# Branch s, the output projection and the feed-forward by two groups of 516 tokens; gate and up tile together as a 2x2 block product of seven; the down projection in two parts

## The chip, the cores and the metric

The kernel runs on one core of one Trainium2 chip. The metric is the device time of one execution in microseconds (us), as the median of several runs. Names of engines as the profile has them: PE (TensorE matmul), PEld (its weight loads), DVE (VectorE), ACT (ScalarE), POOL (GpSimd), SP (SyncE, which issues the DMAs here).

## What is computed

One decoder layer for 1024 prompt tokens and 8 sample tokens, float32, width 1024. Cut to what the change touches:

```python
z = x @ w_in                              # branches a (RG-LRU), s (window attention), c (memory attention), gates g
merged = sum(gates[:, :, n] * (br @ w_branch[n]) for n, br in enumerate((a_out, s_out, c_out)))
h = layer_norm(ALPHA * x + merged @ w_out, ln1_g, ln1_b)
gt, up = jnp.split(h @ w_gate_up, 2, axis=-1)            # 2816 + 2816 features: 22 + 22 tiles of 128
h = layer_norm(ALPHA * h + (jax.nn.silu(gt) * up) @ w_down, ln2_g, ln2_b)
```

## The kernel before, in words

Activations lie transposed: features on the 128 partitions, the T = 1032 tokens (1024 + 8) along the columns. A tile of features by all tokens is thus 128 x 1032. To keep float32 accuracy each operand is split into a high part (ACT casts it, L71) and a low part (DVE subtracts, L72), and each product of a 128x128 weight block with some columns is three matmuls: high x high, high x low, low x high (`mm3`, L105 to L107). Weights come as halves of 128 x 512 floats through a ring of six raw buffers (`half_raw`, SP issues the DMA), and are split into a ring of five high and four low halves (`half_pair`).

The front half, `project`, computes `x @ w_in` in 30 units. Each unit takes two tiles of 128 features as a 2x2 block product with seven products in place of eight (`fast_quarter`, `fast_step`, L244 to L246): the blocks are two halves of the input features and two halves of the tokens, and the pieces are 258 columns wide. While memory attention and window attention run, the branch products of a and c are filled in between as jobs (`branch`, `product`). These products go by three chunks of columns, CH = 384, 384 and 264.

The back half, about 1076 us into the span, works as follows before the change.

- *Branch s* (`brs`, L105 to L107): eight output tiles, each 8 weight blocks x 3 terms x 3 chunks. Its operands `bs` are read back from DRAM (`scr_s`) into slots of their own, so that they can be loaded and split while branch c still runs. Each result is gated, added to M and split (`mH`, `mL`).
- *Output projection* (`out_proj`, `op`): chunk by chunk over all eight tiles, with `wout` split once and kept (`resident`). The first layer norm (`n1`) of a chunk runs in two steps inside the next chunk: the column mean by a matmul with ones (`col_mean`), eight differences (L906), eight squares on ACT and seven sums (L910), a second mean, the root on ACT (L914), the reciprocal (L917), eight scalings (L919). `emit` then writes high and low part of h (L1022, L1023).
- *Feed-forward* (`ffn`): in parts of 8, 7 and 7 feature tiles. For each tile and chunk a gate product (`fg`), tanh, an up product (`fu`) and their product, split into `gH`, `gL`, which stay in memory until the part's down product (`d`) adds them to `acc`. The last part's down weights are resident; there the second layer norm (`n2`) runs chunk by chunk, the last one in a form of its own (`last_layer_norm`, `dl`), which shifts the mean out by small matmuls (`shift`, L959, L960).

A tile framework builds the program: code order gives the order of each engine, with moves by a scheduler, and pools decide when a buffer is free. The order rows below show its outcome.

Of the kernel before, what the change touches and what calls it, by code (L numbers as in the profile page):

```python
# [18 lines left out]
P = 128  # L19
D = 1024  # L20
# [8 lines left out]
FPARTS = ((0, 8), (8, 7), (15, 7))  # L29
NORM_AT = (0, 3)  # L30
LATE = 4
LAST_CH = ((0, 0, 384), (1, 0, 384), (2, 0, 264))
# [9 lines left out]
)  # L42
THIRDS = ((0, 344), (344, 344), (688, 344))
# [10 lines left out]
class Builder:  # L54
# [72 lines left out]
    def setup(self):  # L127
# [10 lines left out]
        nc.vector.memset(self.shift.bitcast(F32), -2.0 / 256)  # L138
# [445 lines left out]
    def product(self, step, br, m, c, wb, gate):  # L584

        nc = self.nc
        t0, n = CH[c]
        ps = self.mm_tile(wb, self.act[br], c, f"br{br}{m}_{c}")
        t = gate[:, t0:t0 + n]
        dst = self.M[m][:, t0:t0 + n]  # L590
        if step == 0:
            nc.vector.scalar_tensor_tensor(dst, t, 1.0, ps, op0=ALU.add, op1=ALU.mult)
            return
        nc.vector.scalar_tensor_tensor(t, t, 1.0, ps, op0=ALU.add, op1=ALU.mult)
        nc.vector.tensor_add(dst, dst, t)
        if step == 2:
            hi, lo = (self.slot(e, c, f"m{e}{m}_{c}", 0) for e in "HL")
            self.split(hi, lo, dst)
            self.merged[m][c] = (hi, lo)
# [262 lines left out]
    def resident(self, src, nk, name, which):  # L862

        nc = self.nc
        raws = [self.half_raw(src[:, o:min(o + 512, nk * P)], min(512, nk * P - o), f"{name}r{o}")
                for o in range(0, nk * P, 512)]
        out = []
        for c in range(3):
            k0, k1 = 3 * c, min(3 * c + 3, nk)
            n = (k1 - k0) * P  # L870
            hi, lo = (self.slot(e, c, f"{name}{e}{c}", which, n) for e in "HL")
            for e, raw in enumerate(raws):
                a, b = max(k0, 4 * e), min(k1, 4 * e + 4)
                if a < b:
                    o = slice((a - k0) * P, (b - k0) * P)
                    self.split(hi[:, o], lo[:, o], raw[:, (a - 4 * e) * P:(b - 4 * e) * P])
            out += [(hi[:, i * P:(i + 1) * P], lo[:, i * P:(i + 1) * P]) for i in range(k1 - k0)]
        return out

    def mm_res(self, w, act, c, name, tag="mm"):  # L880
        n = CH[c][1]
        ps = self.bank(tag, name)
        self.mm3(ps[:, :n], [(w[k], act[k][c]) for k in range(len(w))])
        return ps[:, :n]

    def col_mean(self, s, n, name):

        nc = self.nc
        hi = self.ph.tile([P, 384], F32R, tag="lh", name=f"{name}h", bufs=1)[:, :n]
        lo = self.ph.tile([P, 384], F32R, tag="ll", name=f"{name}l", bufs=1)[:, :n]  # L890
        self.split(hi, lo, s)
        ps = self.bank("o", f"{name}p")[:, :n]
        nc.tensor.matmul(ps, self.ones, hi, start=True, stop=False)
        nc.tensor.matmul(ps, self.ones, lo, start=False, stop=True)
        return ps

    def layer_norm(self, c, r, s1, gcol, emit, name, late=False):


        nc, ph = self.nc, self.ph  # L900
        n = r[0].shape[1]
        yield
        mu = self.col_mean(s1, n, f"{name}mu{c}")
        s2 = ph.tile([P, 384], F32, tag="s2", name=f"{name}s2{c}", bufs=1)[:, :n]
        for m in range(KT):
            nc.vector.tensor_sub(r[m], r[m], mu)  # L906
            sq = s2 if m == 0 else ph.tile([P, 384], F32, tag="sq", name=f"{name}sq{c}_{m}", bufs=2)[:, :n]
            nc.scalar.activation(sq, r[m], AF.Square)
            if m:
                nc.vector.tensor_add(s2, s2, sq)  # L910
        yield
        var = self.col_mean(s2, n, f"{name}va{c}")
        rs = ph.tile([P, 384], F32, tag="rs", name=f"{name}rs{c}", bufs=1)[:, :n]
        nc.scalar.activation(rs, var, AF.Sqrt, bias=self.vec[:, V_EPS:V_EPS + 1])  # L914
# [16 lines left out]

    def last_layer_norm(self, n, r, product, gcol, emit):


        nc, ph = self.nc, self.ph
        ones = self.ones.bitcast(F32)
        tile_ = lambda tag, name, bufs, dt=F32: ph.tile([P, 384], dt, tag=tag, name=name, bufs=bufs)[:, :n]
        s1, s2 = tile_("s1", "ls1", 1), tile_("s2", "ls2", 1)
        hi, lo = (ph.tile([P, n], F32R, tag=f"c0{e}", name=f"c0{e}", bufs=1) for e in "hl")
        e1, e2 = self.bank("t", "le1")[:, :n], self.bank("t", "le2")[:, :n]  # L940

        def account(m):
            sq = s2 if m == 0 else tile_("sq", f"lsq{m}", 2)
# [10 lines left out]
        for m in range(KT):  # L954
# [6 lines left out]
            nc.vector.scalar_tensor_tensor(r[m], ps, 0.5, r[m], op0=ALU.mult, op1=ALU.add)  # L961
            if m == 1:
                s = tile_("xres", "lc0", 3)
                nc.vector.tensor_add(s, r[0], r[1])
                self.split(hi, lo, s)
            elif m == LATE - 1:
# [4 lines left out]
                for k in range(LATE):  # L971
                    nc.vector.scalar_tensor_tensor(r[k], c0, 0.5, r[k], op0=ALU.mult, op1=ALU.add)
# [7 lines left out]
        mu, rs = tile_("xres", "lmu", 3), tile_("gt", "lrs", 3)  # L980
# [12 lines left out]
    def out_proj(self, merged):  # L993
        nc, io, ph = self.nc, self.io, self.ph
        self.accs = [self.acc.tile([P, T], F32, tag="acc", name=f"acc{m}", bufs=8) for m in range(KT)]
        h = [[None] * 3 for _ in range(KT)]
        self.norm = None
        w = [None] * KT
        for c, (t0, n) in enumerate(CH):
            s1 = ph.tile([P, 384], F32, tag="s1", name=f"o1s{c}", bufs=1)[:, :n]  # L1000
            rs = []
            for m in range(KT):
                if c == 0:
                    w[m] = self.resident(io["wout"][m], KT, f"wo{m}", 1)
                ps = self.mm_res(w[m], merged, c, f"op{m}_{c}", tag=("mm", "s")[m % 2])
                if m in NORM_AT:
                    self.norm_step()
                xr = ph.tile([P, 384], F32, tag="xres", name=f"xres{m}_{c}", bufs=3)[:, :n]
                nc.sync.dma_start(xr, io["xT"][:, m, t0:t0 + n])
                nc.scalar.mul(xr, xr, ALPHA)  # L1010
                r = self.accs[m][:, t0:t0 + n]
                nc.vector.scalar_tensor_tensor(r, ps, 0.5, xr, op0=ALU.mult, op1=ALU.add)  # L1012
                if m == 1:
                    nc.vector.tensor_add(s1, rs[0], r)
                elif m > 1:
                    nc.vector.tensor_add(s1, s1, r)
                rs.append(r)

            def emit(m, v, c=c):
                bias = self.vec[:, V_B1 + m:V_B1 + m + 1]  # L1020
                hi, lo = (self.slot(e, c, f"h{e}{m}_{c}", 0) for e in "HL")
                nc.scalar.activation(hi, v, AF.Identity, bias=bias)  # L1022
                nc.vector.scalar_tensor_tensor(lo, v, bias, hi.bitcast(F32), op0=ALU.add, op1=ALU.subtract)  # L1023
                nc.gpsimd.tensor_scalar(v, v, bias, ALPHA, op0=ALU.add, op1=ALU.mult)
                h[m][c] = (hi, lo)
# [252 lines left out]
```

## Time and profile before

| | |
|---|---|
| median of 3 runs | 2028.45 us (2027.67, 2028.92, 2028.45) |
| span of the profiled execution | 2027.6 us |
| busy PE, DVE, ACT, POOL | 1963.3, 1204.2, 879.1, 125.3 us |
| mean granted clock of PE | 0.991 |
| branch c ends, branch s begins | 1075.93, 1077.21 us |
| last product of the down projection begins | 2010.25 us |

The page gives busy times of one execution. A PE that is 97% busy says that matmuls bound the whole; which of them, and what a pause costs, stands in the windows, the waits and the timeline. In a timeline row the columns are start, duration, engine, line, operation, output from inputs, shape and count, and in brackets the idle time before and what ended it. Durations of neighbouring matmuls overlap, so the pace is read from start to start.

### The profile page before, as it was taken

The page shows a single profiled execution, that of the slowest core. Times are in us where ns is not written, and L with a number is a line of the kernel's source. Part 1 is how long each engine was busy: PE and PEld are TensorE (multiplying, and loading weights), DVE is VectorE, ACT ScalarE, POOL GpSimd, SP SyncE. Part 2 cuts the span into 40 slices and gives each one's busy share as a digit, 9 for nine tenths or more (in the row PEclk, how much of TensorE's full clock was granted, in tenths as well). Part 3 has the DMA queues.
Part 4 walks back from the last instruction along what each step waited for, and adds up shares of the span by engine and source line. Part 5 has one row for each costly group of instructions (what it writes and reads, how often), then busy time and mean ns, then how long its engine had stood idle before and what let it go on. Part 6 is the DMA issues. An engine that isn't in the chain of part 4 may idle for free.

```text
span 2027.6 us, 35380 instructions
## 1 busy us (share of the span) xinstructions
PE 1963.3 (97%) x13732; PEld 1930.0 (95%) x13732; DVE 1204.2 (59%) x2565; ACT 879.1 (43%) x1922; POOL 125.3 (6%) x164
## 2 busy tenths in 40 slices
PE   6899999999999999999999999999999999999997
PEld 5899999999999898988999999999999999999996
DVE  8597888777676555389886568533322332223357
ACT  5456565555656455388774244422201221122324
POOL 3000010100000000012110003100000000000001
PEclk8999999999999999999999999999999999999999
DMA  4365455462333676567525241111211111111102
GB/s 173 129 227 181 153 186 170 144 228 82 118 131 114 234 240 215 158 170 204 155 72 174 85 145 30 43 42 43 58 47 43 42 57 41 57 45 43 56 28 84
DMA packets 140439, 235.41 MB, mean 116 GB/s; under 512 B 17280, under 2 KB 69584, under 8 KB 140240
## 3 DMA queue, kind: packets, MB, share of 16 engines
q1 hardware_dynamic: 140272, 233.17, 36.2%
q8 instruction: 107, 1.75, 0.4%
q14 instruction: 60, 0.49, 0.1%
HBM read 179.95 MB, written 55.23 MB: 116 GB/s over the span
## 4 chain that ended last, share of the span: by engine, by line
PE 86%; DVE 6%; DMA 3%; ACT 3%; issue 1%; SPq 0%; ACTq 0%; DVEq 0%; POOL 0%; POOLq 0%
PE ub L245 5%; PE ub L244 5%; PE ub L246 5%; PE fg L105 4%; PE fg L106 4%; PE fg L107 4%; PE fu L107 4%; PE fu L105 4%; PE fu L106 4%; PE d L105 3%; PE d L107 3%; PE d L106 3%; PE ud L246 2%; PE ud L245 2%; PE ud L244 2%; PE brs L105 1%
## 5 line engine op out<-in xcount | busy, mean ns | idle before, releaser
L105 PE MATMUL fg<-hH,wfg_h 128*128 128x384 f32 (+1 forms) x528 | 168.3, 319 | 3.0 <-DVE acc L1012 1.7
L106 PE MATMUL fg<-hL,wfg_h 128*128 128x384 f32 (+1 forms) x528 | 167.7, 318 | 0.4 <-DVE hL L1023 0.4
L107 PE MATMUL fu<-hH,wfu_l 128*128 128x384 f32 (+1 forms) x528 | 167.7, 318 | 0.0
L106 PE MATMUL fu<-hL,wfu_h 128*128 128x384 f32 (+1 forms) x528 | 167.6, 317 | 0.0
L105 PE MATMUL fu<-hH,wfu_h 128*128 128x384 f32 (+1 forms) x528 | 167.5, 318 | 0.0
L107 PE MATMUL fg<-hH,wfg_l 128*128 128x384 f32 (+1 forms) x528 | 167.5, 317 | 0.0
L1041 DVE TENSOR_TENSOR ft<-ft,fu 128x384 f32<-128x384 f32 (+1 forms) x66 | 33.8, 513 | 139.1 <-PE fu L107 139.1
L105 PE MATMUL d<-gH,wd_h 128*128 128x384 f32 (+1 forms) x360 | 114.4, 318 | 0.0
L106 PE MATMUL d<-gL,wd_h 128*128 128x384 f32 (+1 forms) x360 | 114.2, 317 | 0.0
L107 PE MATMUL d<-gH,wd_l 128*128 128x384 f32 (+1 forms) x360 | 114.2, 317 | 0.0
L1039 DVE SCALAR_TENSOR_TENSOR ft<-ft,fg 128x384 f32<-128x384 f32 (+1 forms) x66 | 33.8, 513 | 135.2 <-ACT ft L1038 132.9
L71 ACT CAST gH<-ft 128x384 fp32r<-128x384 f32 (+1 forms) x66 | 31.7, 481 | 175.0 <-DVE ft L1041 175.0
L105 PEld LDWEIGHTS fg<-hH,wfg_h 128*128 128x128 f32 x528 | 99.1, 188 | 3.9 <-DVE acc L1012 2.0
L106 PEld LDWEIGHTS fg<-hL,wfg_h 128*128 128x128 f32 x528 | 99.2, 188 | 1.0 <-DVE hL L1023 0.9
L107 PEld LDWEIGHTS fg<-hH,wfg_l 128*128 128x128 f32 x528 | 99.3, 188 | 0.0
L107 PEld LDWEIGHTS fu<-hH,wfu_l 128*128 128x128 f32 x528 | 99.2, 188 | 0.0
L105 PEld LDWEIGHTS fu<-hH,wfu_h 128*128 128x128 f32 x528 | 99.2, 188 | 0.0
L106 PEld LDWEIGHTS fu<-hL,wfu_h 128*128 128x128 f32 x528 | 99.2, 188 | 0.0
L1061 DVE SCALAR_TENSOR_TENSOR acc<-d,acc 128x384 f32<-128x384 f32 (+1 forms) x48 | 24.8, 516 | 108.4 <-PE d L107 108.4
L1038 ACT ACTIVATE ft<-fg 128x384 f32<-128x384 f32 (+1 forms) x66 | 30.1, 456 | 134.8 <-PE fg L107 134.8
L244 PE MATMUL ub<-th,u_0h 128*128 128x258 f32 x240 | 69.4, 289 | 7.5 <-ACT th L71 6.1
L244 PE MATMUL ud<-th,u_1h 128*128 128x258 f32 x240 | 70.2, 293 | 6.3 <-ACT u_1h L71 5.2
(957 smaller groups left out, 6872.4 us busy)
## 6 DMA issues: line engine op xcount, KB each, us to landing
ur<-win SPq DMA_DIRECT2D x120, 256.0 KB, 3.6
dck<-cmk SPq DMA_DIRECT2D x32, 256.0 KB, 3.6
dcv<-cmvT SPq DMA_DIRECT2D x32, 256.0 KB, 4.5
st<-scr_q SPq DMA_DIRECT2D x32, 256.0 KB, 5.2
scr_g<-za SPq DMA_DIRECT2D x12, 516.0 KB, 5.8
scr_g<-zb SPq DMA_DIRECT2D x12, 516.0 KB, 3.7
x<-xQ SPq DMA_DIRECT2D x8, 516.0 KB
scr_a<-ge SPq DMA_DIRECT2D x8, 516.0 KB
```

The lines of the kernel that those rows point to most:

```text
L71: ins = self.nc.scalar.copy(hi, src).ins
L105: nc.tensor.matmul(ps, sh, mh, start=i == 0, stop=False)
L106: nc.tensor.matmul(ps, sh, ml, start=False, stop=False)
L107: self.last_mm = nc.tensor.matmul(ps, sl, mh, start=False, stop=closes and i == last).ins
L244: mm(sh[:, w], xh, start=opens and k == 0, stop=False)
L245: mm(sh[:, w], xl, start=False, stop=False)
L246: self.last_mm = mm(sl[:, w], xh, start=False, stop=k == 3).ins
L1038: nc.scalar.activation(t, pg, AF.Tanh, scale=0.5)
L1039: nc.vector.scalar_tensor_tensor(t, t, 1.0, pg, op0=ALU.add, op1=ALU.mult)
L1041: nc.vector.tensor_mul(t, t, pu)
L1061: nc.vector.scalar_tensor_tensor(a, ps, 0.5, a, op0=ALU.mult, op1=ALU.add)
```

## The change

Everything up to branch c keeps its order on PE. Branch c's result is now added into two tiles H[0] and H[1] of 8 x 516 columns, one for each group of tokens, so `product` cuts a chunk at column 516. After branch c the memory of its operands and of the gates is given back, and two new pools open there: `arena`, 56 equal slots of 128 x 516 for all split operands, and `late`, for everything else.

- `branch_group(g)`: branch s for one group. It loads and splits its eight operand rows (`load_rows`, tiles `bs`), then goes through eight tiles; `streamed` loads and splits the weights (`sw`) by halves of four blocks, for each group again, and runs two quarters of 258 columns. The sum with the gated result goes to POOL for six of eight tiles.
- `out_group(g)`: the output projection of that group, also with streamed weights. The order is branch 0, projection 0, branch 1, projection 1. The first layer norm of group 0 (`n10`) runs in steps inside branch 1 (after tiles 0 and 3), its block combinations (`h_combos(0)`) inside projection 1. Those of group 1 (`n11`, `h_combos(1)`) run inside the first entry of gate and up.
- `h_combos(p)`: for a group, the seven right-hand operands of the block product, as 14 tiles of 516 columns, each split into high and low part; four combinations by DVE and four by POOL.
- `gate_up`: the gate tile and the up tile of the same 128 features are one 2x2 block product of seven: 7 products x 4 blocks x 3 terms for each group (`ffn_step`, L1064 to L1066). It goes by entries: features 0 and 1 for group 0, the same again for group 1 (their weights are loaded again), then features 2 to 21 for both groups. The product of tanh gate and up is stored to DRAM (`scr_f`).
- `down`: the activations come back from DRAM (`down_rows`, tiles `fg`). First features 0 to 5 for all four quarters, then features 6 to 21 for quarters 0 and 1 together, then for quarter 2, then for quarter 3; the weights of the second part are loaded and split three times. The second layer norm of group 0 (`n20`) runs inside the pass of quarter 2, that of quarter 2 (`n21`) inside the pass of quarter 3, and the last one at the end. The factor 0.5 moves from the sums into the product, the shift becomes -1/256.

The core of the diff:

```diff
-FPARTS = ((0, 8), (8, 7), (15, 7))
+FIRST = 6
+GROUPS = 2
+ENTRIES = ((0, (0,)), (1, (0,)), (0, (1,)), (1, (1,))) + tuple((f, (0, 1)) for f in range(2, NF))
...
+    def wide(self, name):
+        return self.arena.tile([P, HT], F32R, tag="u", name=name, bufs=56)
...
+    def streamed(self, src, nk, acts, pss):
+        for k0 in range(0, nk, 4):
+            n = min(4, nk - k0)
+            w = self.weights(src[:, k0 * P:(k0 + n) * P], n * P, f"sw{self.seq()}_")
+            for c, ps in enumerate(pss):
+                for j, (sh, sl) in enumerate(w):
+                    k = k0 + j
+                    mh, ml = acts[k][c]
+                    nc.tensor.matmul(ps, sh, mh, start=k == 0, stop=False)
+                    nc.tensor.matmul(ps, sh, ml, start=False, stop=False)
+                    self.last_mm = nc.tensor.matmul(ps, sl, mh, start=False, stop=self.closes and k == nk - 1).ins
...
+    def ffn_step(self, st, i, ps_of, names):
+        for p in ps_of:
...
+            for k in range(4):
+                w, o = slice(k * P, (k + 1) * P), slice((k % 2) * QN, (k % 2 + 1) * QN)
+                xh, xl = (a[:, o] for a in self.ht[p][i][k // 2])
+                mm(sh[:, w], xh, start=opens and k == 0, stop=False)
+                mm(sh[:, w], xl, start=False, stop=False)
+                self.last_mm = mm(sl[:, w], xh, start=False, stop=k == 3).ins
...
+    def gate_up(self):
+        ahead = 3
...
+            self.ffn_step(st[e], i, ENTRIES[e][1], str(e))
+            if e == 0 and i in NORM_AT:
+                self.norm_step()
+            if (e, i) == (0, 4):
+                for _ in self.h_combos(1):
+                    pass
...
+    def down(self, rows):
+        for m in range(KT):
+            fetch(2)
+            accumulate(m, 0, FIRST, (0, 1, 2, 3), True, ("mm", "s"))
...
+        for m in range(KT):
+            fetch(2)
+            accumulate(m, FIRST, NF, (0, 1), False, ("mm", "s"))
+            self.add_up(s1, rs, m, nc.gpsimd if m < 6 else nc.vector)
+        self.norm_start(self.layer_norm(rs, s1, V_G2, emitter(0, HT), "n20"))
+        for m in range(KT):
+            accumulate(m, FIRST, NF, (2,), False, (("mm", "s")[m % 2],))
+            if m in NORM_AT:
+                self.norm_step()
```

The order on PE where branch c ends and branch s begins, before (`bsH` and `bsL` are the operands' high and low parts of one chunk, `wbs` the weights of a tile):

```order
L107 MATMUL brc_2_14075<-bcH_2_12457,wbc_l 128x264
L105 MATMUL brs_0_14116<-bsH_0_14008,wbs_h 128x384 [waits Activation_49]
L105 MATMUL brs_0_14161<-bsH_0_14008,wbs_h 128x384 [waits DVE_49]
L106 MATMUL brs_0_14116<-bsL_0_14009,wbs_h 128x384 [waits DVE_49]
L107 MATMUL brs_0_14116<-bsH_0_14008,wbs_l 128x384
L105 MATMUL brs_0_14116<-bsH_0_14013,wbs_h 128x384 [waits Activation_49]
```

And after (`bs_0h` is the high part of the first of eight operand rows of group 0, `sw` a streamed half of weights):

```order
L108 MATMUL brc_2_14043<-bcH_2_12462,wbc_l 128x264
L890 MATMUL brs_0_0_14121<-bs_0h,sw_0_h 128x258 [waits Activation_49]
L890 MATMUL brs_0_1_14122<-bs_0h,sw_0_h 128x258 [waits DVE_49]
L890 MATMUL brs_1_0_14192<-bs_0h,sw_0_h 128x258 [waits DVE_49]
L891 MATMUL brs_0_0_14121<-bs_0l,sw_0_h 128x258 [waits DVE_49]
L892 MATMUL brs_0_0_14121<-bs_0h,sw_0_l 128x258
L891 MATMUL brs_0_1_14122<-bs_0l,sw_0_h 128x258
L892 MATMUL brs_0_1_14122<-bs_0h,sw_0_l 128x258
L891 MATMUL brs_1_0_14192<-bs_0l,sw_0_h 128x258
```

The place is the same; PE now takes three outputs through each operand row before it goes on to the next row, where before it went through the rows for one output.

The order on DVE around the last step of the first layer norm in the feed-forward, before (chunk 2; `ft` is the feed-forward's product):

```order
L72 TENSOR_TENSOR n1va2l<-n1s_16162,n1va2h 128x264 [waits Activation_49]
L917 RECIPROCAL n1rs_16258<-n1rs_16258 128x264 [waits Activation_49]
L1041 TENSOR_TENSOR ft_1_16309<-ft_1_16309,fu_1_16312 128x384 [waits DVE_49,PE_49]
L919 SCALAR_TENSOR_TENSOR acc_15042<-acc_15042,vec,n1rs_16258 128x264 [waits DVE_49]
L919 SCALAR_TENSOR_TENSOR acc_15043<-acc_15043,vec,n1rs_16258 128x264
L919 SCALAR_TENSOR_TENSOR acc_15044<-acc_15044,vec,n1rs_16258 128x264
L1023 SCALAR_TENSOR_TENSOR hL_2_16263<-acc_15042,vec,hH_2_16262 128x264 [waits Activation_49]
```

And after (group 1; H is the group's tile, `t` a combination, `hl` and `hh` the split operands, `u` the weights of an entry's seven products, `us` their block sums):

```order
L987 RECIPROCAL n11rs<-n11rs 128x516 [waits Activation_49]
L73 TENSOR_TENSOR u_2l<-us_2_16827,u_2h 128x512
L989 SCALAR_TENSOR_TENSOR H_8861<-H_8861,vec,n11rs 128x516 [waits DVE_49]
L989 SCALAR_TENSOR_TENSOR H_8861<-H_8861,vec,n11rs 128x516 x7
L1016 TENSOR_TENSOR t_16752<-H_8861 128x516 [waits Activation_49]
L73 TENSOR_TENSOR u_3l<-ur_01_16618,u_3h 128x512 [waits DMAHW2_49,PE_49]
L1016 TENSOR_TENSOR t_16754<-t_16752,H_8861 128x516 [waits DVE_49]
L73 TENSOR_TENSOR hl_0_0_16733<-H_8861,hh_0_0_16732 128x516 [waits Activation_49]
L1016 TENSOR_TENSOR t_16760<-H_8861 128x516
L73 TENSOR_TENSOR hl_0_1_16737<-H_8861,hh_0_1_16736 128x516 [waits Activation_49]
L1016 TENSOR_TENSOR t_16762<-t_16760,H_8861 128x516 [waits DVE_49]
L73 TENSOR_TENSOR hl_1_0_16743<-t_16740,hh_1_0_16742 128x516 [waits Activation_49]
```

The norm's operations are now 516 columns wide, combinations and splits of them follow, and splits of weights that the products of group 0 need (`u_2l`, `u_3l`) stand in the same queue between them.

More of the change, by code (lines that the diff above doesn't have):

```diff
@@ L589, in product @@
         t = gate[:, t0:t0 + n]
[L590 to L599, printed above, removed]
+        if step:
+            nc.vector.scalar_tensor_tensor(t, t, 1.0, ps, op0=ALU.add, op1=ALU.mult)
+        for g in range(GROUPS):
+            a, b = max(t0, g * HT), min(t0 + n, (g + 1) * HT)
+            if a >= b:
+                continue
+            dst = self.H[g][:, m, a - g * HT:b - g * HT]
+            if step:
+                nc.vector.tensor_add(dst, dst, gate[:, a:b])
+            else:
+                nc.vector.scalar_tensor_tensor(dst, gate[:, a:b], 1.0, ps[:, a - t0:b - t0], op0=ALU.add, op1=ALU.mult)
     def branch(self, step, br):
@@ L891, in col_mean @@
         self.split(hi, lo, s)
[L892 to L900, printed above, removed]
+        out = []
+        for c in range(0, n, QN):
+            ps = self.bank("ot"[c // QN], f"{name}p{c}")[:, :QN]
+            nc.tensor.matmul(ps, self.ones, hi[:, c:c + QN], start=True, stop=False)
+            nc.tensor.matmul(ps, self.ones, lo[:, c:c + QN], start=False, stop=True)
+            out.append((slice(c, c + QN), ps))
@@ L991, in last_layer_norm @@
             emit(m, r[m], self.vec[:, gcol + m:gcol + m + 1])
[L993 to L1025, printed above, removed]
-            self.norm_start(self.layer_norm(c, rs, s1, V_G1, emit, "n1"))
-        return h
```

357 lines of the change are left out of this document (243 added, 114 removed).

## The prediction, made before the changed kernel ran

> **What bounds the kernel now.** I read the page first: the share of each engine, and the chain that ended last.
>
> ```profile
> PE 1963.3 (97%) x13732; PEld 1930.0 (95%) x13732; DVE 1204.2 (59%) x2565; ACT 879.1 (43%) x1922; POOL 125.3 (6%) x164
> PE 86%; DVE 6%; DMA 3%; ACT 3%; issue 1%; SPq 0%; ACTq 0%; DVEq 0%; POOL 0%; POOLq 0%
> ```
>
> TensorE is the bound. Next I cut the back half, the only part that changes much, into windows. The columns are length, then busy time (and instructions) of PE, PEld, DVE, ACT, POOL, then the granted clock, the DMA share and GB/s. The windows are branch s, the output projection, most of the feed-forward, its last passes, and the tail.
>
> ```profile
> 1076.00:1166.00 90.00, 89.00 (x566) 88.46 (x565) 56.44 (x117) 31.43 (x70) 0.00 (x0) 1.00 0.40 132
> 1166.00:1258.00 92.00, 91.85 (x585) 91.56 (x584) 67.68 (x130) 42.18 (x87) 11.02 (x11) 1.00 0.32 96
> 1258.00:1960.00 702.00, 698.68 (x4448) 697.10 (x4448) 240.28 (x459) 154.04 (x306) 12.28 (x13) 1.00 0.16 47
> 1960.00:2010.00 50.00, 50.00 (x340) 49.85 (x340) 41.26 (x78) 19.85 (x38) 4.18 (x5) 1.00 0.09 32
> 2010.00:2028.00 18.00, 3.18 (x13) 1.51 (x11) 12.59 (x23) 9.61 (x20) 4.93 (x6) 0.74 0.42 148
> ```
>
> From 1076 to 2010 PE hardly pauses. The list of waits, cut to PE, names every pause of that stretch, and one long pause ahead of it (bra).
>
> ```profile
> PE bra L105 <- ACT baH L71: 5.0, 1, 5.0
> PE fg L105 <- DVE acc L1012: 1.7, 1, 1.7
> PE fg L105 <- ACT hH L1022: 1.3, 1, 1.3
> PE brs L105 <- ACT bsH L71: 1.0, 1, 1.0
> PE le L976 <- DVE ls L950: 0.7, 1, 0.7
> PE le L978 <- DVE acc L961: 0.6, 1, 0.6
> PE fg L106 <- DVE hL L1023: 0.4, 1, 0.4
> ```
>
> Without bra they sum to 5.7 us. So the back half costs its matmuls and almost nothing else: what the change saves in matmuls counts in full, and so does every new wait. The front half keeps its instructions; branch c gets a few more small DVE additions, at a place where PE has other work. I cost that at nothing.
>
> **The matmuls.** Pairs from the timeline give the start-to-start time: 258 columns (45 matmuls apart), 264 columns (23 apart), 384 columns (18 apart).
>
> ```profile
> 318.66 0.28 PE L246 MATMUL ub<-th,u_0l 128*128 128x258 f32 x1
> 324.03 0.28 PE L246 MATMUL ub<-th,u_2l 128*128 128x258 f32 x1
> ...
> 1073.13 0.28 PE L105 MATMUL brc<-bcH,wbc_h 128*128 128x264 f32 x1
> 1075.93 0.28 PE L107 MATMUL brc<-bcH,wbc_l 128*128 128x264 f32 x1
> ...
> 1264.53 0.33 PE L107 MATMUL fg<-hH,wfg_l 128*128 128x384 f32 x1
> 1267.65 0.34 PE L107 MATMUL fg<-hH,wfg_l 128*128 128x384 f32 x1
> ```
>
> They are 0.1193, 0.1217 and 0.1733 us. A row of 1032 columns takes 2 x 0.1733 + 0.1217 = 0.4683 us in three chunks and 4 x 0.1193 = 0.4772 us in four quarters. Before, branch s and the projection have 64 weight blocks each, gate and up 352, down 176: 656 blocks x 3 terms x 0.4683 = 921.6 us (measured from 1075.93 to the last product at 2010.25: 934, of which 5.7 are the waits and some 5 the small mean matmuls, so this sum closes to a few us). After, branch s and projection take 768 matmuls each, down 2112, and gate and up 22 tiles x 7 products x 4 blocks x 3 terms x 2 groups = 3696: 7344 x 0.1193 = 876.1 us. **Gain 45.5 us**: about 52 from seven products in place of eight, 6 given back by the narrower pieces.
>
> By the rows a matmul costs about 9 ns beside its columns (0.1217 and 0.1733 lie 120 columns and 0.0516 us apart: 0.43 ns a column, 0.1135 for 264). The Trainium skill, "TensorE: Matmul & The Clock Gate", section "Back-to-back issue gap", has 2.5 ns there; by it four quarters would cost only 0.6% more than three chunks and the gain would be some 3 us larger. The rows decide.
>
> **What a pause costs.** Ahead of branch a, PE waited 5.03 us.
>
> ```profile
> 681.43 0.69 PE L105 MATMUL bra<-baH,wba_h 128*128 128x384 f32 x1 [5.03 <-ACT baH L71]
> 682.51 0.52 PE L107 MATMUL bra<-baH,wba_l 128*128 128x384 f32 x1
> 686.35 0.52 PE L107 MATMUL bra<-baH,wba_l 128*128 128x384 f32 x1
> 687.53 0.34 PE L107 MATMUL bra<-baH,wba_l 128*128 128x384 f32 x1
> ...
> 1263.54 0.44 PE L105 MATMUL fg<-hH,wfg_h 128*128 128x384 f32 x1 [1.70 <-DVE acc L1012]
> 1263.83 0.34 PE L106 MATMUL fg<-hL,wfg_h 128*128 128x384 f32 x1
> ```
>
> From 682.51 to 686.35 twelve matmuls took 0.32 us each, not 0.173; then the rate came back. Some sixteen slow ones lose 2.4 us more. After 1.70 us (the last two rows) nothing is lost. So I add up to 2.4 us to a wait of over about 4 us, and nothing below 2. The same page, section "Part 1: The HAM clock gate", says an idle window of about 3.4 us halves the clock and about 3.4 us of work restores it. The row agrees in kind and shows 5 us of slow work; by the page each such pause would lose 1.7 us.
>
> **New pauses.** They hang on DVE, whose rates come from these rows: a 512-column split, then pairs of 384 and of 264 columns (two operations apart), then two reciprocals.
>
> ```profile
> 1287.68 0.68 DVE L72 TENSOR_TENSOR wfg_l<-wfg1r__16400,wfg_h 128x512 fp32r<-128x512 f32 x1
> 1288.29 0.89 DVE L72 TENSOR_TENSOR wfg_l<-wfg1r__16406,wfg_h 128x512 fp32r<-128x512 f32 x1
> ...
> 1242.46 0.55 DVE L906 TENSOR_TENSOR acc<-acc,n1mu1p 128x384 f32<-128x384 f32 x1
> 1243.39 0.55 DVE L906 TENSOR_TENSOR acc<-acc,n1mu1p 128x384 f32<-128x384 f32 x1
> ...
> 1270.65 0.42 DVE L906 TENSOR_TENSOR acc<-acc,n1mu2p 128x264 f32<-128x264 f32 x1
> 1271.34 0.42 DVE L906 TENSOR_TENSOR acc<-acc,n1mu2p 128x264 f32<-128x264 f32 x1
> ...
> 1249.75 2.55 DVE L917 RECIPROCAL n1rs<-n1rs 128x384 f32<-128x384 f32 x1 [0.70 <-ACT n1rs L914]
> 1277.37 1.80 DVE L917 RECIPROCAL n1rs<-n1rs 128x264 f32<-128x264 f32 x1 [1.24 <-ACT n1rs L914]
> ```
>
> 512 columns take 0.61 us, 384 take 0.465, 264 take 0.345; on that line 516 take 0.60 and 258 take 0.34. A reciprocal grows by 0.75 us over 120 columns: 3.4 us for 516.
>
> - *Gate and up, first entries (the largest term).* The second group's layer norm and the 14 splits of its block combinations have nothing finished to hide behind but the two entries of group 0. From the split of its mean (n11ml) to the first weight split of the fourth entry, DVE's list holds 45 operations of 516 columns, 23 of 512, 11 of 258 and one reciprocal: 27.0 + 14.0 + 3.7 + 3.4 = 48.1 us. DVE also waits for the mean and for the root, 1.8 and 1.2 us by the like rows of before (the second stands in the reciprocal row above): 51. PE issues 234 matmuls meanwhile, 28 us. The difference is 23 us; followed wait by wait I find 25 (four of nearly 5 us, for u_5l, u_3l, u_4l and u_6l, the rest shorter). I take 25. The low end is 18, where PE still has older work when the list begins; the high end 35, if ACT's casts, one ahead of each split, hold DVE up too.
> - *Branch c to branch s.* The rows bs of group 0 take the memory that branch c's operands leave, so their loads start about 1 us before c ends. Load to landing is a few us, then a cast:
>
> ```profile
> bsL<-scr_s SPq DMA_DIRECT2D x16, 192.0 KB, 3.8
> ur<-win SPq DMA_DIRECT2D x120, 256.0 KB, 3.6
> ```
>
>   That gives 4 us (1.0 before; bra's 5.0 is the nearest row from above, so 1 to 7). SP's queue holds the first gate load and the weights behind these rows; branch s alone waits for them. The gate sums that go to POOL are needed only by the projection, up to eight steps later: nothing.
> - *Layer norm of group 0 inside branch s of group 1.* DVE needs there, in each of 8 steps, 4 weight splits, 2 multiplications and a split, 3.7 us, and two additions at the end: 31 us; the norm's 15 differences and sums, 2 splits, 8 scalings (25 x 0.60) and the reciprocal take 18.4 more. That is 49 us against 384 x 0.1193 = 46 of PE, and the norm comes in two lumps: 5 (0 to 9).
> - *Gate and up to down.* Rows of group 1 are loaded back behind the last stores on SP: a landing of 3.6 less what runs: 2 (0 to 5).
> - *Layer norm of groups 0 and 1's first half in the passes by quarters.* A half weight now lasts 12 x 0.1193 = 1.43 us on PE, and only 4 low halves fit: 4.3 to 5.7 us of cover against 9.0 us of norm operations in a row, then 8.2 (reciprocal and eight scalings): 7 (2 to 12).
> - *Starts of the projections and the second norm of the passes:* 2 (0 to 5).
>
> Together 45 us in place of 5.7: +39. For slow matmuls after the long ones: 2 at branch s, 1 at the norm, 1.5 in gate and up (there DVE sets the pace and hides most), 3.5 in the passes: +8 (0 to 14). The mean matmuls grow from 20 to 28: +1.
>
> **The tail.** Before, the last product ends behind scalings of the previous chunk:
>
> ```profile
> 2010.25 0.28 PE L960 MATMUL dl<-c0l,shift 128*128 128x264 f32 x1
> 2011.11 1.62 DVE L919 SCALAR_TENSOR_TENSOR acc<-acc,vec,n2rs 128x384 f32<-128x384 f32 x2
> 2012.65 0.42 DVE L961 SCALAR_TENSOR_TENSOR acc<-dl,acc 128x264 f32<-128x264 f32 x1
> 2019.32 0.51 DVE L919 SCALAR_TENSOR_TENSOR acc<-acc,vec,n2rs 128x384 f32<-128x384 f32 x1
> ```
>
> The addition waits from 2010.5 to 2012.65 and one more scaling takes 0.44. The previous quarter is now 258 columns wide and its scalings come sooner: -2.5 (0 to -4).
>
> **The sum.** 2027.6 - 45.5 + 39 + 8 + 1 - 2.5 = 2027.6. That is against the profiled span, 0.85 us below the median of the runs, 2028.45. The runs thus read 2028.5; I add 1.5 us for waits below 1 us that I did not list and forecast **2030 us: no change** that a measurement can tell (0.2%, 4 us; 2024.4 to 2032.5).
>
> **Rivals.**
> - *The pauses are mostly covered.* For it: the scheduler puts splits between norm operations, and before, the same norm cost only 3.4 us. Against: then two finished chunks, 768 columns, lay ready; now nothing does. With 3, 1, 19, 1, 3 and 1 us for the pauses and 3 for slow matmuls: 2027.6 - 45.5 - 5.7 + 28 + 3 + 1 - 2.5 + 0.85 = 2007. Chance 0.28.
> - *Slower: the weights do not come fast enough in the passes by one quarter.* Each of 64 half weights must come every 1.43 us through 6 raw buffers, so a buffer may be held 8.6 us from issue to the end of its split. Landing took 3.6, the splits 1.2; DVE's norm lumps or a landing near bra's 5.0 use the rest. If a half comes every 2.0 us, the two passes lose 64 x 0.57 = 36 us: 2066. The 183 GB/s that this needs lie above the 132 of branch s, for it; that branch s did not ask for more speaks against. Chance 0.14.
> - *Slower: ACT is the second pace-maker.* Each low split waits for a cast that ACT queues behind squares, biases and the tanh. If that takes the first entries to their high end, 35, and the norms in branch s and in the passes to 9 and 12: +19, 2049. ACT's 43% speak against. Chance 0.14.
>
> **How the numbers follow.** The forecast has 0.44, with 2016 to 2044 as its own range (the largest term alone spans 17); of it 0.11 falls below 2024.4, 0.21 in the band, 0.12 above. Faster: 0.28 + 0.11 = 0.39. Same: 0.21. Slower: 0.14 + 0.14 + 0.12 = 0.40. For 8 in 10 the range reaches from 2004, inside the first rival, to 2056, between the two last.
>
> **What would show it.** After: L1064 to L1066 about 441 us apart for 3696 matmuls of 0.119; waits of about 5 us on u_5l, u_3l, u_4l and u_6l, 25 us together, with DVE full; 4 us before brs; 2 waits on sw in the pass of the third quarter; the clock below 1 behind the long ones. I am wrong if the waits of the back half sum to under 30 or over 60 us, or if the 258-column rate is not 0.119.

## The result, and the profile after

The changed kernel takes 2050.08 us (median of 4 runs, 2048.7 to 2053.35) against 2028.68 before (4 runs on the same chip): ratio 1.0101, 95% interval 1.0087 to 1.0115. It is slower by 1%, where I had forecast no change. The span is 2047.1 us against 2027.6.

The page of the changed kernel, first the busy time of each engine, then the chain that ended last:

```profile
PE 1947.0 (95%) x15180; PEld 1910.7 (93%) x15180; DVE 1403.4 (69%) x2867; ACT 1024.0 (50%) x2147; POOL 164.9 (8%) x175
PE 36%; DVE 4%; issue 2%; ACT 1%; POOL 1%; DMA 0%; ACTq 0%; DVEq 0%; POOLq 0%
```

The shares of the chain add up to 44%: it reaches back only to about 1175 us, so it tells of the back half alone. PE works 16 us less in a span that is 20 us longer, so PE waits more. DVE has 199 us more to do: in the back half its weight splits grow from 91 to 238 us, since weights are split once for each group or quarter, and the block sums of weights add 66 us. The windows of the changed kernel (columns as before): branch s, projection and again branch s, projection for groups 0 and 1; the first entries of gate and up; the rest of gate and up; the passes of quarters 2 and 3.

```profile
1076.00:1133.00 57.00, 50.23 (x385) 48.83 (x385) 28.35 (x49) 19.33 (x32) 9.69 (x6) 0.94 0.50 157
1133.00:1180.50 47.50, 46.47 (x387) 46.26 (x386) 25.41 (x43) 19.11 (x32) 8.08 (x5) 1.00 0.58 179
1180.50:1237.70 57.20, 50.43 (x395) 50.02 (x394) 45.56 (x67) 28.73 (x47) 10.76 (x7) 0.94 0.36 111
1237.70:1287.00 49.30, 46.60 (x386) 46.18 (x386) 37.18 (x58) 21.91 (x38) 14.39 (x8) 1.00 0.39 119
1287.00:1343.00 56.00, 37.38 (x215) 34.17 (x215) 50.30 (x80) 32.86 (x61) 9.52 (x4) 0.76 0.12 38
1343.00:1763.00 420.00, 420.00 (x3491) 419.94 (x3490) 261.00 (x492) 165.14 (x327) 0.00 (x0) 1.00 0.27 86
1925.00:1985.00 60.00, 51.95 (x394) 51.33 (x393) 46.19 (x75) 33.03 (x56) 0.00 (x0) 0.91 0.57 175
1985.00:2033.00 48.00, 47.99 (x400) 47.78 (x400) 38.93 (x76) 26.67 (x56) 5.80 (x6) 1.00 0.53 159
```

Long stretches are full (420 of 420 us). Four are not, and there the granted clock is below 1 too: the start of branch s, branch s of group 1, the first entries, the pass of quarter 2. In the first entries DVE is busy 50.3 of 56 us and PE 37.4. The longest of PE's waits from branch s on:

```profile
PE d L892 <- DVE sw_l L73: 7.2, 2, 3.8
PE brs L890 <- DVE gts L916: 6.8, 2, 4.2
PE fc L1066 <- DVE u_3l L73: 6.8, 1, 6.8
PE op L890 <- DVE H L938: 3.7, 3, 1.6
PE brs L890 <- ACT bs_0h L72: 3.4, 1, 3.4
PE fd L1066 <- DVE u_5l L73: 3.1, 1, 3.1
PE fb L1064 <- ACT u_4h L72: 2.4, 1, 2.4
PE fb L1066 <- DVE u_6l L73: 2.4, 1, 2.4
```

The whole list sums to 43.6 us, where I had 45; but each wait also has its slow matmuls and the time until the next matmul is under way. Counted by stage from the start times on the timeline, with 0.1203 us a matmul (the small matmuls for the means and the shift are taken off too):

| stage | its time, us | over its matmuls, us | forecast |
|---|---|---|---|
| pause ahead of branch s, and branch s of group 0 | 57.3 | 11.1 | 4 + 2 |
| branch s of group 1, with the first norm of group 0 | 57.2 | 10.0 | 5 + 1 |
| the two projections | 47.5 and 49.3 | 1.3 and 3.1 | 2 |
| gate and up, nearly all in its first entries | 476.2 | 30.6 | 25 + 1.5 |
| start of down, passes of all quarters, of 0 and 1 | 162.0 | 0.3 | 2 |
| passes of quarters 2 and 3 | 60.0 and 47.9 | 12.8 and 0.4 | 7 + 3.5 |
| sum | | 69.6 | 53 |

From the end of branch c to the last product the back half takes 957.4 us where it took 934.3; the tail behind it 13.9 where it took 17.3.

### The profile page after: what moved, and what is told of

It is laid out like the page before. It is cut to its first block, busy times and chain, and to the rows that moved or that the text cites. A ratio compares the mean times of both kernels' runs of the same rounds, so it can differ in the third digit from the quotient of the medians.

```text
span 2047.1 us, 39560 instructions
## 1 busy us (share of the span) xinstructions
PE 1947.0 (95%) x15180; PEld 1910.7 (93%) x15180; DVE 1403.4 (69%) x2867; ACT 1024.0 (50%) x2147; POOL 164.9 (8%) x175
## 5 line engine op out<-in xcount | busy, mean ns | idle before, releaser
L890 PE MATMUL d<-fg_0h,sw_h 128*128 128x258 f32 x352 | 99.7, 283 | 0.0
L892 PE MATMUL d<-fg_0h,sw_l 128*128 128x258 f32 x352 | 99.6, 283 | 0.0
L891 PE MATMUL d<-fg_0l,sw_h 128*128 128x258 f32 x352 | 99.6, 283 | 0.0
L229 DVE TENSOR_TENSOR us<-ur,ur 128x512 f32<-128x512 f32 x108 | 74.3, 688 | 3.0 <-DMA ur<-wgu 1.6
L890 PE MATMUL op<-mh,sw_h 128*128 128x258 f32 x256 | 72.6, 284 | 3.7 <-DVE H L938 3.7
L229 DVE TENSOR_TENSOR us<-us,ur 128x512 f32<-128x512 f32 x108 | 74.5, 690 | 2.4
L246 PE MATMUL ud<-tl,u_1h 128*128 128x258 f32 x240 | 70.4, 294 | 3.0 <-DVE tl L73 3.0
L892 PE MATMUL op<-mh,sw_l 128*128 128x258 f32 x256 | 72.4, 283 | 0.0
L891 PE MATMUL op<-ml,sw_h 128*128 128x258 f32 x256 | 72.3, 282 | 0.0
L247 PE MATMUL ud<-th,u_1l 128*128 128x258 f32 x240 | 70.4, 295 | 0.7 <-DVE u_1l L73 0.7
```

What stands on the lines that cost most here:

```text
L229: nc.vector.tensor_add(src, a, b)
L246: mm(sh[:, w], xl, start=False, stop=False)
L247: self.last_mm = mm(sl[:, w], xh, start=False, stop=k == 3).ins
L890: nc.tensor.matmul(ps, sh, mh, start=k == 0, stop=False)
L891: nc.tensor.matmul(ps, sh, ml, start=False, stop=False)
L892: self.last_mm = nc.tensor.matmul(ps, sl, mh, start=False, stop=self.closes and k == nk - 1).ins
```

## The experiments

Theory A after the result: where a norm runs, DVE's list is longer than PE's matmuls, and PE waits for the weight splits behind it. Rival B: the narrow pieces and the streamed weights cost the time by themselves. Stages are told in us of the timeline (start to start), since the front half, which no edit touches, ends within a range of 4 us over these runs (1074.5 to 1078.4).

| kernel | span | ahead of branch s + branch s 0 | branch s 1 | projection 1 | gate, up | pass of q 2 |
|---|---|---|---|---|---|---|
| changed | 2047.1 | 57.3 | 57.2 | 49.3 | 476.2 | 60.0 |
| first norm left out | 2007.8 | 58.5 | 45.8 | 49.2 | 451.5 | 57.5 |
| sums on POOL | 2049.5 | 60.0 | 55.6 | 49.3 | 479.3 | 58.8 |
| four by group | 2050.2 | 57.9 | 57.8 | 49.3 | 479.3 | 57.5 |
| small steps | 2049.9 | 58.4 | 56.8 | 49.3 | 475.2 | 62.1 |
| rows first | 2041.9 | 51.1 | 55.7 | 49.3 | 476.2 | 59.9 |
| nothing on POOL | 2042.4 | 57.9 | 54.3 | 46.1 | 474.2 | 61.2 |
| lean norms | 2035.5 | 58.0 | 53.5 | 49.3 | 468.8 | 55.5 |
| the last three together | 2016.9 | 51.0 | 50.3 | 46.1 | 467.6 | 54.4 |
| the same with small steps | 2021.9 | 51.3 | 49.1 | 46.1 | 467.6 | 57.2 |

All but the changed kernel and the last two are single executions; seven runs of the kernel before, beside the later ones, lie between 2028.0 and 2034.4 us. Untouched stages move by up to 3 us from run to run, so less than that in one stage, taken alone, shows nothing.

**The first norm left out.**

```diff
-        self.norm_start(self.layer_norm(rs, s1, V_G1, emit, f"n1{g}"))
```

> The first layer norm of both groups is left out (means, variance, root, scaling and bias), all else stays. Theory A, DVE's list sets the pauses: branch s of group 1 loses about 10 of its 57 us, and the first entries of gate and up lose 25 operations of 516 columns and the reciprocal, 15 + 3.4 us plus the slow scalings, of which about 22 us of PE's 30 us excess: span 2047 - 10 - 22 = 2015. Branch s of group 0 (11 us over its matmuls) and the passes by one quarter (15 us over) stay as they are. Rival B, the narrow pieces and the streamed weights cost the time by themselves: within 5 us of 2047.

The span fell by 39 us, to 2007.8: 11.4 in branch s of group 1, 24.7 in gate and up, 2.5 in the pass of quarter 2, which has nothing of this norm. Branch s of group 1 now takes what its matmuls take (384 x 0.1203 = 46.2), and gate and up is 7 us over its own (3696 x 0.1203 = 444.6). Rival B is out as the main cause: the same streamed weights and narrow pieces run at nearly full pace as soon as the norm is gone. The run takes the norm's work from ACT as well as from DVE, so it does not tell the two apart.

**Block sums on POOL.** In `fast_quarter`, for entries 1 to 3:

```diff
-            nc.vector.tensor_add(src, a, b)
+            (nc.gpsimd if st.get("pool") else nc.vector).tensor_add(src, a, b)
...
+            st[e]["pool"] = 1 <= e < 4
```

> The four block sums of the weights of entries 1 to 3 of gate and up go from DVE to POOL: 12 operations of 512 columns, 7.2 us off DVE's list. Theory A: the first entries take 6 to 7 us less, span 2040. Rival C, ACT's casts set the pace there: no change (2047). Rival D, POOL is slower (its two combinations took 3.2 us each here) and slows DVE beside it: no gain or up to 10 us longer.

Gate and up took 479.3 us, 3 more, which is no more than untouched stages move by. Rival D: taking 7.2 us from DVE by way of POOL gained nothing. In this run the eight scalings of group 1's first norm (L989) took 8.1 us in all, 1084 ns the mean, while POOL was at work beside them; three of them took 1.6 to 1.8 us, the others 0.74:

```profile
L989 DVE SCALAR_TENSOR_TENSOR H<-H,vec,n11rs 128x516 f32<-128x516 f32 x8 | 8.1, 1084 | 0.0
```

That pointed to a cost that I had not in my sum, and I looked for it in the changed kernel itself: DVE rows of branch s of group 1, then the POOL rows beside them.

```profile
1199.26 1.67 DVE L73 TENSOR_TENSOR sw_l<-sw_r__15532,sw_h 128x512 fp32r<-128x512 f32 x1
1200.85 0.68 DVE L73 TENSOR_TENSOR sw_l<-sw_r__15562,sw_h 128x512 fp32r<-128x512 f32 x1
1203.76 1.80 DVE L73 TENSOR_TENSOR sw_l<-sw_r__15663,sw_h 128x512 fp32r<-128x512 f32 x1
```

```profile
1199.09 1.29 POOL L918 TENSOR_TENSOR H<-H,gts 128x516 f32<-128x516 f32 x1 [10.40 <-DVE gts L916]
1203.32 1.69 POOL L918 TENSOR_TENSOR H<-H,gts 128x516 f32<-128x516 f32 x1 [2.94 <-DVE gts L916]
```

Two like splits, 1.67 and 0.68 us: the slow one lies on POOL's addition, and so does that of 1.80. Both of these end 0.55 us behind POOL's addition (1200.93 against 1200.38, 1205.56 against 1205.01): the split was held until POOL had finished.

**Four features by single groups.**

```diff
-ENTRIES = ((0, (0,)), (1, (0,)), (0, (1,)), (1, (1,))) + tuple((f, (0, 1)) for f in range(2, NF))
+ENTRIES = tuple((f, (p,)) for p in range(2) for f in range(4)) + tuple((f, (0, 1)) for f in range(4, NF))
```

> Four features instead of two go by single groups at the start of gate and up, so 40 us of finished group 0 work instead of 20 stand ahead of group 1. If the trouble is that too little finished work lies ready (rival E), the pause shrinks by 15 us or more: span 2032. Theory A: each such entry brings DVE 8.9 us of weight work for PE's 10.1, so two more give only 2 to 3 us of slack: span 2044 to 2047.

Gate and up 479.3: no gain; the 3 us more are again what untouched stages move by. Twice the finished work ahead does not help: DVE is as full there as before (49.8 us from 1287 to 1343 us), which fits that such an entry brings DVE nearly as much as PE. Rival E is out.

**Small steps.** The norm yields behind every second tile, and is advanced behind each half of weights instead of at two tiles:

```diff
+            if m % 2:
+                yield
...
+            self.norm_step()
```

> The norms inside branch s of group 1 and inside the passes by one quarter are issued in steps of two tiles behind each half of weights, instead of in two lumps; the first entries of gate and up are issued as before. Theory F, the lumps outlast the cover of four low halves: the pass of quarter 2 loses 10 of its 15 us over, branch s of group 1 about 5 of 10: span 2032. Rival G, it is DVE's sum in these stages: branch s of group 1 keeps its 10, since 49 us of DVE stand against 46 of PE, and the pass loses little: span 2044.

Branch s of group 1 took 56.8 (57.2), the pass of quarter 2 took 62.1 (60.0) and that of quarter 3 took 50.7 (47.9). I read this as the fall of theory F, but the run does not test it: the smaller steps stand in the code, and the order that DVE ran still has the lumps. In the pass of quarter 2 the reciprocal, the eight scalings and the weight splits beside them lay so in the changed kernel:

```profile
1959.69 3.38 DVE L987 RECIPROCAL n20rs<-n20rs 128x516 f32<-128x516 f32 x1
1962.98 0.63 DVE L73 TENSOR_TENSOR sw_l<-sw_r__24739,sw_h 128x512 fp32r<-128x512 f32 x1
1963.53 5.41 DVE L989 SCALAR_TENSOR_TENSOR H<-H,vec,n20rs 128x516 f32<-128x516 f32 x8
1969.19 0.69 DVE L73 TENSOR_TENSOR sw_l<-sw_r__24757,sw_h 128x512 fp32r<-128x512 f32 x1
```

and with small steps:

```profile
1944.61 3.37 DVE L986 RECIPROCAL n20rs<-n20rs 128x516 f32<-128x516 f32 x1
1948.17 5.41 DVE L990 SCALAR_TENSOR_TENSOR H<-H,vec,n20rs 128x516 f32<-128x516 f32 x8
1953.50 0.69 DVE L73 TENSOR_TENSOR sw_l<-sw_r__24550,sw_h 128x512 fp32r<-128x512 f32 x1
```

The lump grew, since no weight split stands in it any more, and PE's wait behind it went from 3.3 to 5.5 us. Rival G does not stand either: in these two stages of the changed kernel DVE is busy 45.6 of 57.2 us and 46.2 of 60.0, so its sum does not pass PE's 46. What the traces do show is that PE's long waits there end just behind a long row of norm operations on DVE: in the pass on the first weight split after it, in branch s on `gts` (L916), the product that reads a finished tile. That fits theory F, which no run here tests. In branch s the scalings now met POOL's additions more often: three of the eight took 1.6 us or more, in place of one. Two of them took together:

```profile
1207.17 2.46 DVE L990 SCALAR_TENSOR_TENSOR H<-H,vec,n10rs 128x516 f32<-128x516 f32 x2
```

**Rows first.** The first tile's weights are made ahead of the rows, the gates and all other weights behind the eighth row's load, on SP:

```diff
+        made = self.weights(io["wbr"][8], D, "sw0_") if g == 0 else None
+        self.ahead = self.last_load if g == 0 else None
...
+            with self.tc.issue_after(self.row_load) if g == 0 else ExitStack():
+                nc.sync.dma_start(gate, self.scr["g"][:, 8 + m, cols])
+                self.streamed(io["wbr"][8 + m], KT, acts, pss, made if m == 0 else None)
```

> Where branch s of group 0 begins, all eight operand rows are loaded before the gates and before the weights of its second tile. Theory I: in the changed kernel rows 6 and 7 stood behind a weight load on SP that waited for a ring buffer, and the cast of row 4 behind a weight cast on ACT that waited for PE, so that queue order costs 4 of the 11 us over there: branch s of group 0 goes from 53.6 to about 50 us, its gap of 3.7 us ahead stays, span 2043. Rival J, the rows come as fast as the DMA engines bring them: 53 to 54 us, span 2047.

The stage lost 6.2 us, more than I expected: the pause ahead of it, which I had put down to memory, went from 3.7 to 0.3 us, and branch s itself from 53.6 to 50.8. SP's queue shows both, first in the changed kernel, with the sum of its waits for weight splits between 1060 and 1100 us ahead:

```profile
SPq L83 <- DVE sw_l L73: 11.6, 5, 7.1
1075.37 0.33 SPq L83 DMA_DIRECT2D sw_r__14407<-wbr  x1
1075.80 0.38 SPq L876 DMA_DIRECT2D bs_0l<-scr_s  x1
1078.04 0.38 SPq L876 DMA_DIRECT2D bs_1l<-scr_s  x1
1080.37 0.43 SPq L876 DMA_DIRECT2D bs_5l<-scr_s  x1
1087.91 0.33 SPq L83 DMA_DIRECT2D sw_r__14478<-wbr  x1
1088.30 0.42 SPq L876 DMA_DIRECT2D bs_6l<-scr_s  x1
```

and with the rows first (there branch c ended at 1078.06):

```profile
1074.67 0.54 SPq L878 DMA_DIRECT2D bs_0l<-scr_s  x1
1076.42 0.33 SPq L878 DMA_DIRECT2D bs_1l<-scr_s  x1
1080.15 0.43 SPq L878 DMA_DIRECT2D bs_7l<-scr_s  x1
```

In the changed kernel the first row's load left SP just as branch c ended, behind a weight load (`sw_r__14407`) that had stood 3.0 us (from 1072.3 to 1075.3) until a weight split freed its raw buffer. The seventh row (`bs_6l`) stood behind another such load, which left 7.5 us after the sixth row's (`bs_5l`); the wait of 7.1 us in the list is this one. With the rows first the first load leaves 3.4 us before branch c ends. So the memory of the first row was free early enough; the queue was the wait. The next two rows did wait for memory there: their loads left about 1.1 us late each, for products of branch c.

**Nothing on POOL.** The gated sums (L918), the running sums for the mean (L949, L951) and the four combinations go to DVE:

```diff
-            (nc.gpsimd if m < 6 else nc.vector).tensor_add(dst, dst, gate)
+            nc.vector.tensor_add(dst, dst, gate)
...
-            self.add_up(s1, rs, m, nc.gpsimd if m < 6 else nc.vector)
+            self.add_up(s1, rs, m, nc.vector)
```

> All additions and combinations that the back half gives to POOL (except the last norm's) go to DVE. Theory H, POOL's operation holds a DVE operation beside it: a weight split beside a POOL addition took 1.67 to 1.80 us in place of 0.60, so each addition on POOL costs DVE 1.1 us and would cost it 0.60 as its own; branch s of group 1 loses about 4 of its 57 us, the first entries of gate and up 3 to 4 (there a sum also waited 2.25 us for POOL), span 2040. Theory A without contention: DVE gets 6 more additions of 0.6 us in branch s of group 1 and 4 combinations in the first entries, +3.5 and +2.4: span 2053.

DVE got more operations and the kernel got faster, by 4.7 us of span and by 7.1 from the end of branch c to the last product: 2.9 in branch s of group 1, 3.2 in projection 1 (a stage that I had not named), 2.0 in gate and up, 1.2 given back in the pass of quarter 2. Theory H holds in sign and roughly in size. Projection 1 is the clean case: 46.1 us in all three kernels with nothing on POOL, 49.2 or 49.3 in all others. But the edit takes away a second thing too: ACT's cast of a gated sum waited for POOL ten times in the changed kernel, 1.0 to 1.9 us each, with weight casts behind it in ACT's queue. What share of the gain is whose was not tried apart. The eight scalings of group 0, with POOL beside them in the changed kernel:

```profile
1215.11 6.26 DVE L989 SCALAR_TENSOR_TENSOR H<-H,vec,n10rs 128x516 f32<-128x516 f32 x8
```

and with nothing on POOL:

```profile
1215.36 5.41 DVE L989 SCALAR_TENSOR_TENSOR H<-H,vec,n10rs 128x516 f32<-128x516 f32 x8
```

**Lean norms.** PE sums the squares (in one rounded part instead of high and low), ACT scales:

```diff
-            if m:
-                nc.vector.tensor_add(s2, s2, sq)
+            for o, ps in va:
+                nc.tensor.matmul(ps, self.ones, sq[:, o], start=m == 0, stop=m == KT - 1)
...
-            nc.vector.scalar_tensor_tensor(r[m], r[m], self.vec[:, gcol + m:gcol + m + 1], rs, op0=ALU.mult,
-                                           op1=ALU.mult)
-            emit(m, r[m])
+            nc.vector.tensor_mul(r[m], r[m], rs)
+            emit(m, r[m], self.vec[:, gcol + m:gcol + m + 1])
```

> In the norms of the groups and of quarter 2 the sum of the squares is made by PE (each square times ones, summed in PSUM) in place of seven DVE additions and a split, and the scale by the vector moves from DVE into ACT's bias step. DVE's list loses 8 x 0.60 + 8 x 0.19 = 6.3 us a norm, ACT's loses one cast, PE gets 12 small matmuls more (1.4 us). Theory A: branch s of group 1 -4, first entries of gate and up -6, pass of quarter 2 -4: span 2033 to 2036. Rival C, ACT paces: no gain, span 2047 to 2051. PE could also wait at each square in its own queue, up to 5 us a norm: then 2050.

Branch s of group 1 -3.7, gate and up -7.4, pass of quarter 2 -4.5: the forecast of theory A, term by term. ACT has hardly less to do (1021.8 us busy against 1024.0), so its load does not pace: that speaks against rival C here and against ACT as second pace-maker in the prediction. The edit also shortens a lump, in the pass of quarter 2 to eight differences in a row where fifteen differences and sums stood, so it does not tell DVE's sum from the length of the lumps.

**The three together.**

> The three edits of the runs before in one kernel: rows first, nothing on POOL, lean norms. If the terms add: 2047 - 4 - 7 - 13 = 2023, which is 5 us under the kernel before. If POOL's relief of DVE counts for more than its contention: 2035 to 2040.

2020.05 us (4 runs, 2018.75 to 2023.08) against 2030.48 before on the same chip: ratio 0.9952, interval 0.9934 to 0.9971. The edits add up: from the end of branch c to the last product they save 7.4, 7.1 and 14.3 us one by one, 28.8 in all, and 29.8 together. This version beats the kernel before by 0.5%. What remains of the pauses is again in the first entries, and one in the pass of quarter 2:

```profile
PE fb L1070 <- DVE u_2l L73: 5.9, 1, 5.9
PE fc L1070 <- DVE u_3l L73: 5.1, 1, 5.1
PE d L894 <- DVE sw_l L73: 3.6, 1, 3.6
```

**The three with small steps.** The edits of the small steps on top.

> The kernel of the three edits, with the norms inside branch s of group 1 and inside the passes by one quarter once more in steps of two tiles. With nothing on POOL a step no longer holds other DVE work up. If lumps cost what is left there (50.3 us for branch s of group 1 and 54.4 for the pass of quarter 2, each over 46 of matmuls): both fall to about 48, span 2017 - 2 - 6 = 2009. If DVE's sum or the depth of the rings sets them: within 2 us of 2017.

2023.0 us (2020.18 to 2023.85), ratio to before 0.9956 (0.9939 to 0.9972): the same as without. Branch s of group 1 is 1.2 shorter, the pass of quarter 2 is 2.8 longer. In that pass the reciprocal and the eight scalings again run without a weight split between them, where the version without small steps has two splits there, so this run does not clear the lumps either.

## What the prediction had right and wrong, point by point

The forecast of 2030 us, no change, missed by 20 us: the mechanism held in the main, and several terms were too small. That 2050 lies inside the range of 2004 to 2056 is luck, not working: it lies outside the forecast's own 2016 to 2044, at the place of a rival whose mechanism did not come.

- *PE is the bound and new waits count in full:* right. Every stage that was mended gave its time to the span.
- *The matmuls:* counts right, pace wrong, by the prediction's own sign (a rate that is not 0.119). I read 0.1193 us from 45 matmuls in a row. In the changed kernel, from a row in the first feature's entry of group 1 to the first of down, 3455 matmuls lie 415.79 us apart, 0.1203:

```profile
1347.46 0.28 PE L1065 MATMUL fb<-hl,u_6h 128*128 128x258 f32 x1
1763.25 0.29 PE L890 MATMUL d<-fg_0h,sw_h 128*128 128x258 f32 x1
```

  With it the gain is 921.6 - 7344 x 0.1203 = 38 us, not 45.5. Seven of the 20 us that I missed are here. Two side figures are off without entering the sum: by my own numbers the gain parts into 54 and 8 us, not 52 and 6. And worked out with the 2.5 ns of the Trainium skill, "TensorE: Matmul & The Clock Gate", section "Back-to-back issue gap", which gives that figure for an isolated matmul, the gain is by estimate some 8 us larger, not 3.
- *Branch s of group 0:* I gave 4 + 2 for a reuse of memory, and said of SP's queue that branch s alone waits for it. It was 11.1, of which the queue's order was 6.2. The step that failed is "their loads start about 1 us before c ends": I had the place in the order of SP, but did not ask what the weight load ahead of the row waits for. That the pause itself came out at 3.7 us, near the 4 of the forecast, was luck: it came from the queue.
- *POOL:* "needed only by the projection ...: nothing" failed. PE waited for none of these results, but ACT's casts did, and DVE ran slower beside POOL. With nothing on POOL some 7 us went from these stages.
- *The norms:* right that they cost the most, too small, and in branch s of group 1 not for the reason given. I had 49 us of DVE against 46 of PE there; DVE was busy 45.6, and PE's two long waits (2.6 and 4.2 us) each ended behind a long row of the norm's operations. I had 0.60 us for a scaling of 516 columns; it took 0.68 alone (5.41 by 8), and 0.78 and 0.89 in the mean of eight where POOL held up some of them. In the first entries DVE's list ran as written, PE's longest wait (6.8 us, for u_3l) ended behind the eight scalings, and a sum stood 2.25 us behind a combination on POOL:

```profile
1307.27 3.38 DVE L987 RECIPROCAL n11rs<-n11rs 128x516 f32<-128x516 f32 x1 [1.11 <-ACT n11rs L984]
1311.11 7.10 DVE L989 SCALAR_TENSOR_TENSOR H<-H,vec,n11rs 128x516 f32<-128x516 f32 x8
1329.53 0.43 DVE L1075 TENSOR_TENSOR fza<-fc,p1s 128x258 f32<-128x258 f32 x1 [2.25 <-POOL t L1016]
```

  The reciprocal took the 3.4 us of the estimate. Of the four waits of about 5 us that I named, three stand in the list, in other lengths (u_3l 6.8, u_5l 3.1, u_6l 2.4); in place of u_4l stands its high half u_4h, which ACT casts (2.4).
- *Slow matmuls after pauses:* I had 8 us, with 1.5 in the first entries because DVE hides them there. From branch s on 184 matmuls lie 0.16 to 0.25 us behind the one before without a pause between, 17 us lost, 7.4 of them in the first entries. What part of those 7.4 DVE's pace would have taken anyway was not tried apart.
- *The passes:* 7 + 3.5 against 13.2. I argued with lumps against four low halves. The trace fits that: PE's two long waits in the pass of quarter 2 (3.8 and 3.3 us) end on the first weight split behind a lump. But no run tests it: the small steps left the lumps as they were, and the depth of the ring was not tried, for lack of memory in the front half. That fewer DVE operations gave 4.5 us fits as well.
- *The tail:* -2.5 forecast, 17.3 to 13.9 measured, -3.4.
- *Rivals:* 2049 us stood in the list, for a second pace-maker in ACT. The time came, the mechanism did not: the pauses lie behind DVE's lumps, with POOL and SP's queue adding to them. The rival that half weights come too late (2066) did not come either: the pass of quarter 3 runs at the pace of its matmuls.

The sum of what I missed: 7 us of pace and 17 us of pauses (69.6 against 53) one way. The other way go some 2.5 us that the kernel before also lost beside my rows and its list of waits (its matmuls lay 0.1736 and 0.1216 us apart over the back half, and its pauses with the slow matmuls behind them took 7.1 us), 1 us for the small matmuls (38 now take what 30 took before) and 1 in the tail: 7 + 17 - 2.5 - 1 - 1 = 19.5, which is the 2047.1 - 2027.6 = 19.5 us of the spans.

## What to carry to other kernels

When a change cuts matmuls but splits weights anew for each group, write DVE's list for every stage beside PE's, with POOL's operations counted into DVE's list rather than taken off it. Look at its order as well as at its sum: a long row of other work ahead of the one split that PE needs can stop PE though the sums fit. More finished work ahead did not help here, where that work filled DVE nearly as much as PE. When an edit is to change an order, read from the trace that the order changed. Then read each DMA queue for what stands ahead of the loads that a stage begins with. And take a pace from hundreds of matmuls: 1% of 880 us was a third of the miss.

## What the runs showed of the hardware

- DVE operations with two SBUF inputs and operations on POOL hold each other up. The two splits of 512 columns shown above that began inside a POOL addition took 1.67 and 1.80 us and ended 0.55 us behind it; a split that began first took its usual 0.69 (1203.16 in the changed kernel, POOL from 1203.32). The delay is thus what is left of POOL's operation, here 1.0 to 1.2 us, more than the 0.6 that the addition costs on DVE itself. The Trainium skill, "GPSIMD Engine Reference", section "1. Specifications", says that POOL's SBUF interfaces are shared with VectorE and contend with DVE instructions that have two SBUF inputs. The traces agree; that section gives no price.
- A scaling by a vector and a tensor took 0.68 us for 516 columns where a plain product took about 0.61 (eight in 4.93 us in the version of three edits).
- After the pause of 3.4 us ahead of branch s of group 0 matmuls of 258 columns lay 0.21 to 0.22 us apart for some 5 us, in place of 0.12, as in the kernel before; with pauses every few us the clock stayed at a mean of 0.76 over the 56 us of the first entries.
- The pace of 258 columns was 0.1198 us in the front half (mean of the 4889 start-to-start times under 0.13 us in the changed kernel) and 0.1203 in its back half. What makes the 0.4% was not tried.
